# Softmax chain, layer-norm lead and 512-column weight splits in a two-layer decoder trunk

## The chip, the cores and the metric

The kernel runs on one core of one Trainium2 chip. The metric is the device time of one launch in microseconds (us), as the median of several runs. A profiled execution adds a trace; the numbers in the rows below come from that one execution.

## The reference

Two layers over one sequence of 512 tokens with 1024 features, all float32. Cut to what is computed:

```python
u = rmsnorm(x, g_pre)                                   # layer 0
z, xbc, dt_raw, q, k, v, f_raw = split(u @ e_w_in)      # 1024 x 7200
xbc = silu(causal_depthwise_conv(xbc, conv_w) + conv_b) # 4 taps -> xs, B, C
y = ssd_chunked(xs, dt, a, B, C) + xs * d_skip          # 4 groups, chunks of 128
y = group_rmsnorm(y * silu(z_ssd)) * ssd_norm
o = softmax(q k^T / 8 + c_t - c_s, causal) @ v          # 16 heads of 64
x = x + rmsnorm(concat(y, o * silu(z_fox)) @ e_w_out, g_post)

u = rmsnorm(x, g_pre)                                   # layer 1
val, gate, z = split(u @ o_w_in)                        # 1024 x 6144
h = causal_depthwise_conv(val * sigmoid(gate), w31) + b # 31 taps, 2048 channels
h = silu(layernorm(h, g, b)) * silu(z)
x = x + rmsnorm(h @ o_w_out, g_post)
```

## The kernel before

**Every product is made of three matmuls.** Each float32 operand is split in a rounded part (type fp32r, "hi") and the remainder ("lo"); `mm3` (L109) sums hi*hi, hi*lo and lo*hi. The rounding is a copy on ScalarE (ACT) and the remainder a subtract on VectorE (DVE) or GpSimd (POOL): `split` (L117) and `hilo` (L121).

**Weight jobs.** The two input projections and the two output projections are a list of jobs, each with 1024 columns' worth of weights in a 128x1024 tile. A job's weights go through three steps: `wload` (L159) loads a raw tile, of which there are two, with a DMA issued on SyncE's queue (SP); `cast` (L151) rounds it on ACT (L155 or L157 in the profile); a subtract on `j.eng` (L119 in the profile, tile name `w`) makes the lo part. `split_to` (L246) does this at priority offset 100 for the jobs up to two ahead of the running one, more where the dictionary `ahead` has an entry. A job's weights lie in a tile of pool `q` (7 buffers), or, where `j.small` is set, in four 128x512 tiles of pool `t` (56 buffers). By default jobs alternate between DVE and POOL; jobs 6 to 39 are all given to POOL (L1486), and jobs 0 to 3 are split before that. The 48 weight jobs of layer 1's input projection have their lo parts made long before, by `lo_ahead` (L190): load to `pre`, round on ACT to `prh` (L204), subtract on DVE (L205), store to DRAM. That filler is spread over layer 0 and its tiles are 128x1024.

**What sets the order.** TensorE (PE) runs its instructions in the order written. The queues of DVE, ACT and POOL are filled by the Tile framework's planner: it steps through a modelled time and takes, among the instructions that it holds ready on an engine, the one that is earliest in the program, with `tc.high_priority(offset=n)` counted as n places earlier. On the chip each queue then runs strictly in that order, so an instruction whose input is late holds back all that stand behind it. `HP` is 601 and is used before the change for the short convolution's taps, the SSD segments and some PSUM copies, not for attention.

**Layer 0.** Jobs 0 to 2 (B, C and x of group 0) run in two halves of 256 tokens as the tokens' norm comes in (L1094 to L1119). Then z and the other projections run; `Steps` (L270) puts SSD and attention steps between their matmuls when enough modelled PE time has passed since their inputs (DL, L1214, and the numbers in `attention`). In SSD, `bc_parts` (L1226) makes hi and lo of B and C, which `cbT` (L1267, PE tile `cb`) multiplies; later `states`, `state_parts` and `yoff` (PE tile `yo`) carry the state over chunks, and `gate_scale` (L1359, DVE L1362) feeds the transposes `yT`. In attention, for each of 16 heads and 4 query blocks, `sa` (L1421) writes logits to a PSUM bank `s`, then DVE takes the negated row maximum `nmx` (L1431), ACT the exponential with its row sum (tile `pr`, shown as L95), DVE the reciprocal `ri` (L1436), and POOL multiplies (L1437). `sb` (L1441) transposes that on PE (`pT`), and a split on ACT and DVE (`ph`, `pl`) feeds `sc`, the product with v. `sb` may follow `sa` after 8 us of modelled PE time. All eight PSUM banks come from one pool.

**Layer 1.** After the convolution 16 tiles of results lie in SBUF (`cvo`). The last three jobs of the input projection are z jobs of 24 matmuls each (tiles 13 to 15). `stats1` (L1032) stands before them: sums over channels on PE (`st`), mean and rstd on DVE and POOL, and diagonal tiles `dm` (L1049). `run(NZ[0])` runs some z jobs, `stats2` (L1051) broadcasts mean and rstd to two PSUM banks (`mu`, `rs`), `leads[1]()` runs the lead-in, and `run(NZ[1])` runs the z jobs left. NZ is [2, 1]. Then the output projection `out_proj` (L611) takes the 16 tiles in order (8 jobs for columns 0 to 511, of two tiles each, then 8 for the rest). Each tile goes through `lnorm` (DVE L1061 and L1062, then Silu on ACT), `lgate` (POOL L1067) and `hilo` (ACT, then DVE, tile `hll`). LA, LB and LC say how many tiles each of the three stages is ahead of PE; the lead-in fills them to that depth.

Of the kernel before, what the change touches and what calls it, by code (L numbers as in the profile page):

```python
# [36 lines left out]
def trunk(  # L37
# [21 lines left out]
    ctx.enter_context(tc.manual_schedule(engines={mybir.EngineType.PE}))  # L59

    HP = 601
    LA = 5
    LB = 4
    LC = 2
    NZ = [2, 1]
    GLO = [3, 11]
    uid = [0]

# [48 lines left out]
    def split(hi, lo, src, hi_eng, lo_eng):  # L117
        hi_eng(hi, src)
        lo_eng.tensor_tensor(lo, src, f32(hi), ALU.subtract)  # L119
# [57 lines left out]
    def wsplit(j):  # L177
        _, _, nk, _, n = j.spec
        hl = j.hl if j.lo is not None else wtiles(j.small)
        w = 1024 // len(hl[0])  # L180
        for i in range(len(hl[0])):
            src = j.raw[:, i * w : (i + 1) * w]
            if j.lo is not None:
                cast(hl[0][i], src)
            else:
                split(hl[0][i], hl[1][i], src, cast, j.eng)
        m = w // n
        return [lambda k, t=t: t[k // m][:, k % m * n : (k % m + 1) * n] for t in hl]

    def lo_ahead(js):  # L190


        def load(j):
            w, r0, nk, c0, n = j.spec
            t = ep.tile([P, 1024], F32, tag="e", name=nm("pre"))
            with tc.issue_after(last_load[0]):
                nc.sync.dma_start(t.rearrange("p (k f) -> p k f", k=nk),
                                  w[r0 : r0 + nk * P, c0 : c0 + n].rearrange("(k p) f -> p k f", p=P))
            return t

        def sub(t):
            h = eh.tile([P, 1024], F32R, tag="eh", name=nm("prh"))
            with tc.issue_after(last_cast[0]):
                A.copy(h, t)  # L204
            V.tensor_tensor(t.bitcast(F32R), t, f32(h), ALU.subtract)  # L205

        def store(j, t):
            j.lo = lop.tile([P, 1024], F32, tag="lo", name=nm("lo"))
            nc.sync.dma_start(j.lo, t)
        loaded = []  # L210
        for i in range(len(js) + 2):
            if i > 1:
                sub(loaded[i - 2])
            if i > 2:
                store(js[i - 3], loaded[i - 3])
            if i < len(js):
                loaded.append(load(js[i]))
            yield
        store(js[-1], loaded[-1])
# [869 lines left out]
        if b == 2:  # L1089
            load_to(2)  # L1090
    load_columns()
    jobs[0].eng, jobs[1].eng = V, G
    with tc.issue_after(mark["sq"]), tc.issue_after(mark["rstd"]), tc.issue_after(mark["scale"]):
        split_to(1)  # L1094
    to_uT(uh, ul, 0, us[0:2], c0)
# [129 lines left out]

    def bc_parts(g):  # L1226
        st = SG[g]
        st["B"] = hilo(st["Bf"], eng=G)
        st["C"] = hilo(st.pop("Cf"), eng=G)

    def x_tokens(g, i):

# [184 lines left out]
    def attention(steps):  # L1417
# [3 lines left out]
        def sa(h, i):  # L1421
# [5 lines left out]
            mm(ps[:, :L], QS[:, qs], KS[:, :L], True, False)  # L1427
            mm(ps[:, :L], QX[0:68, qs], KX[0:68, :L], False, False)
            mm(ps[:, L - P : L], identb, maskq, False, True)
            nmx = col("nmx")  # L1430
            V.tensor_reduce(nmx, ps[:, :L], AX.X, ALU.max, negate=True)  # L1431
            p = pr[h, i] = t2("pr")
            rs = col("rs")
            act(p[:, :L], ps[:, :L], AF.Exp, bias=nmx, accum_out=rs)
            ri = col("ri")
            V.reciprocal(ri, rs)  # L1436
            G.tensor_scalar(p[:, :L], p[:, :L], ri, 1.0, ALU.mult, ALU.mult)  # L1437
            if i == NB - 1:
                del qk["q", h], qk["k", h]

        def sb(h, i):  # L1441
# [4 lines left out]
            for kb in range(i + 1):  # L1446
                tr(pb[:, tok(kb)], p[:, tok(kb)], ident)
            src = pb.rearrange("p (k q) -> p k q", k=NB)[:, : i + 1, :]
            split(ph[h][:, : i + 1, tok(i)], pl[h][:, : i + 1, tok(i)], src, A.copy, V)

        def sc(h):
            po = bank("o")
# [51 lines left out]
        jobs[J1 + i].eng = V if i % 2 else G  # L1504
    for i in range(8):
        ahead[J1 - 8 + i] = max(2, min(NSMALL, 3 + 2 * (i - 2)) + 7 - i)
    run(J1 - state["run"])
    for _ in early:
        pass
# [59 lines left out]
```

## Time and profile before

| what | value |
|---|---|
| runs | 957.57, 959.45, 960.0 us; median 959.45 |
| the profiled execution | 954.4 us, its span 952.5 us, mean granted clock 0.989 |
| PE busy | 911.9 us (96%) |
| DVE busy | 736.3 us (77%) |
| ACT busy | 594.5 us (62%) |
| POOL busy | 503.3 us (53%) |
| HBM read, written | 129.45 MB, 29.36 MB |

The span runs from the first to the last instruction; the 1.9 us around it belong to the execution's own time. The profiled execution is 5.05 us shorter than the median of the runs. Matmuls are pipelined: a record of 0.39 us is the life of one matmul, and the pace is read from how many start in a stretch. [...]

### The profile page before, as it was taken

The page shows a single profiled execution, that of the slowest core. Times are in us where ns is not written, and L with a number is a line of the kernel's source. Part 1 is how long each engine was busy: PE and PEld are TensorE (multiplying, and loading weights), DVE is VectorE, ACT ScalarE, POOL GpSimd, SP SyncE. Part 2 cuts the span into 40 slices and gives each one's busy share as a digit, 9 for nine tenths or more (in the row PEclk, how much of TensorE's full clock was granted, in tenths as well). Part 3 has the DMA queues.
Part 4 walks back from the last instruction along what each step waited for, and adds up shares of the span by engine and source line. Part 5 has one row for each costly group of instructions (what it writes and reads, how often), then busy time and mean ns, then how long its engine had stood idle before and what let it go on. Part 6 is the DMA issues. An engine that isn't in the chain of part 4 may idle for free.

```text
span 952.5 us, 13693 instructions
## 1 busy us (share of the span) xinstructions
PE 911.9 (96%) x4691; PEld 757.7 (80%) x4691; DVE 736.3 (77%) x1220; ACT 594.5 (62%) x1073; POOL 503.3 (53%) x425
## 2 busy tenths in 40 slices
PE   5998999998999999989899999999999999998997
PEld 5976787886798888878678889888888887776885
DVE  5776967899887797968866257899999989769703
ACT  5547566575864766667585346788786778545500
POOL 2516443633632543434473202898999999458510
PEclk9999999999999999989999999999999999999999
DMA  6636522347774475664527793654664763513413
GB/s 186 193 106 198 169 75 67 89 133 243 222 241 135 134 245 187 190 200 138 173 90 243 243 367 152 189 165 146 221 208 136 231 188 124 170 72 133 147 52 110
DMA packets 180265, 159.83 MB, mean 168 GB/s; under 512 B 7708, under 2 KB 151716, under 8 KB 180196
## 3 DMA queue, kind: packets, MB, share of 16 engines
q1 hardware_dynamic: 180180, 158.96, 52.0%
q8 instruction: 37, 0.61, 0.2%
q14 instruction: 32, 0.26, 0.1%
q10 hardware_dynamic: 16, 0.00, 0.0%
HBM read 129.45 MB, written 29.36 MB: 167 GB/s over the span
## 4 chain that ended last, share of the span: by engine, by line
PE 69%; DVE 11%; issue 6%; ACT 5%; POOL 4%; DMA 3%; SPq 1%; DVEq 0%; POOLq 0%; ACTq 0%
PE m L102 39%; PE o L102 17%; PE tm L102 5%; POOL w L119 3%; DMA wr<-in_e_w_in_dram 2%; PE s L102 2%; DVE pre L205 2%; ACT w L157 2%; DVE hll L119 2%; PE pT L106 1%; PE yd L102 1%; PE acc L102 1%; DVE w L119 1%; DVE cvo L1062 1%; DVE cvo L1061 1%
## 5 line engine op out<-in xcount | busy, mean ns | idle before, releaser
L102 PE MATMUL m<-uh,w 128*128 128x512 f32 (+1 forms) x1392 | 452.7, 392 | 1.8 <-POOL w L119 1.8
L102 PEld LDWEIGHTS m<-uh,w 128*128 128x128 f32 x1392 | 260.8, 189 | 52.8 <-issue 3.1
L102 PE MATMUL m<-ul,w 128*128 128x512 f32 (+1 forms) x696 | 267.0, 384 | 0.0
L119 POOL TENSOR_TENSOR w<-wr,w 128x1024 fp32r<-128x1024 f32 x61 | 150.3, 2467 | 188.5 <-ACT w L157 151.0
L963 DVE SCALAR_TENSOR_TENSOR acc<-h,cw,acc 128x490 f32<-128x490 f32 (+14 forms) x272 | 177.6, 726 | 5.4 <-ACT acc L955 4.5
L102 PE MATMUL o<-w,hlh 128*128 128x512 f32 x512 | 160.9, 396 | 1.3 <-ACT pr L95 1.2
L870 POOL TENSOR_TENSOR acc<-acc,prod 128x505 f32<-128x505 f32 (+12 forms) x122 | 156.4, 1284 | 9.2 <-ACT prod L856 1.8
L102 PEld LDWEIGHTS m<-ul,w 128*128 128x128 f32 x696 | 132.0, 190 | 20.8 <-issue 0.5
L102 PEld LDWEIGHTS o<-w,hlh 128*128 128x128 f32 x512 | 94.5, 189 | 20.6 <-ACT pr L95 1.7
L102 PE MATMUL o<-w,hll 128*128 128x512 f32 x256 | 100.9, 394 | 4.9 <-DVE hll L119 4.9
L205 DVE TENSOR_TENSOR pre<-pre,prh 128x1024 fp32r<-128x1024 f32 x48 | 75.0, 1563 | 38.6 <-ACT prh L204 26.9
L157 ACT CAST w<-wr 128x1024 fp32r<-128x1024 f32 x72 | 75.1, 1048 | 46.3 <-DMA wr<-in_e_w_out_dram 18.8
L1437 POOL TENSOR_SCALAR pr<-pr,ri 128x128 f32<-128x128 f32 (+1 forms) x64 | 41.7, 653 | 104.4 <-DVE ri L1436 84.3
L102 PE MATMUL tm<-w,uh 128*128 128x256 f32 (+1 forms) x384 | 94.3, 337 | 1.7 <-ACT pr L95 1.7
L155 ACT CAST w<-wr 128x1024 fp32r<-128x1024 f32 x60 | 62.0, 1049 | 30.6 <-DMA wr<-in_o_w_out_dram 17.0
L856 ACT ACTIVATE prod<-h,cw 128x505 f32<-128x505 f32 (+12 forms) x122 | 77.7, 708 | 0.0
L102 PEld LDWEIGHTS tm<-w,uh 128*128 128x128 f32 x384 | 64.9, 196 | 7.6 <-ACT pr L95 1.9
L341 POOL TENSOR_TENSOR rstd<-var,mhalf 128x1 f32<-128x1 f32 (+1 forms) x20 | 12.8, 642 | 103.3 <-DVE var L339 103.1
L204 ACT CAST prh<-pre 128x1024 fp32r<-128x1024 f32 x48 | 50.4, 1050 | 21.5 <-DVE pre L205 19.6
L102 PE MATMUL tm<-w,ul 128*128 128x256 f32 (+1 forms) x192 | 62.5, 326 | 0.0
L102 PEld LDWEIGHTS o<-w,hll 128*128 128x128 f32 x256 | 48.4, 189 | 17.2 <-DVE hll L119 7.3
L95 ACT ACTIVATE pr<-s,nmx 128x128 f32<-128x128 f32 (+1 forms) x64 | 33.8, 529 | 36.3 <-DVE nmx L1431 22.9
(263 smaller groups left out, 1564.9 us busy)
## 6 DMA issues: line engine op xcount, KB each, us to landing
wr<-in_e_w_in_dram SPq DMA_DIRECT2D x56, 512.0 KB
pre<-in_o_w_in_dram SPq DMA_DIRECT2D x48, 512.0 KB
lo<-pre SPq DMA_DIRECT2D x48, 512.0 KB
wr<-in_o_w_in_dram SPq DMA_DIRECT2D x48, 512.0 KB
w<-lo SPq DMA_DIRECT2D x44, 512.0 KB
wr<-in_e_w_out_dram SPq DMA_DIRECT2D x16, 512.0 KB
wr<-in_o_w_out_dram SPq DMA_DIRECT2D x16, 512.0 KB
x<-in_x_dram SPq DMA_DIRECT2D x12, 256.0 KB
```

Source lines behind the costliest of these rows:

```text
L95: i = A.activation(*a, **kw)
L102: T.matmul(o, l, r, start=start, stop=stop, skip_group_check=True)
L119: lo_eng.tensor_tensor(lo, src, f32(hi), ALU.subtract)
L155: last_cast[0] = A.copy(hi, src).ins
L157: last_cast[0] = A.copy(hi, src).ins
L204: A.copy(h, t)
L205: V.tensor_tensor(t.bitcast(F32R), t, f32(h), ALU.subtract)
L341: mark["rstd"] = G.tensor_tensor(r, v, mhalf.to_broadcast([P, ss.shape[-1]]), ALU.pow).ins
L856: A.activation(prs[i][:, s:], hs[j][:, : S - s], AF.Copy, scale=w31(30 - s, j))
L870: G.tensor_tensor(a2[j][:, s:], a2[j][:, s:], prs.pop(i)[:, s:], ALU.add)
L963: V.scalar_tensor_tensor(a[:, s:], h[:, : S - s], w31(30 - s, j), a[:, s:], ALU.mult, ALU.add)
L1437: G.tensor_scalar(p[:, :L], p[:, :L], ri, 1.0, ALU.mult, ALU.mult)
```

## The change

```diff
-    LA = 5
-    LB = 4
-    LC = 2
-    NZ = [2, 1]
+    LA = 6
+    LB = 5
+    LC = 3
+    NZ = [1,2]
...
             else:
-                split(hl[0][i], hl[1][i], src, cast, j.eng)
+                cast(hl[0][i], src)
+                for c in range(0, w, S if j.eng is G else w):
+                    sl = slice(c, c + (S if j.eng is G else w))
+                    j.eng.tensor_tensor(hl[1][i][:, sl], src[:, sl], f32(hl[0][i])[:, sl], ALU.subtract)
...
         def sub(t):
             h = eh.tile([P, 1024], F32R, tag="eh", name=nm("prh"))
-            with tc.issue_after(last_cast[0]):
-                A.copy(h, t)
-            V.tensor_tensor(t.bitcast(F32R), t, f32(h), ALU.subtract)
+            for i in range(2):
+                sl = slice(i * S, i * S + S)
+                with tc.issue_after(last_cast[0]):
+                    A.copy(h[:, sl], t[:, sl])
+                V.tensor_tensor(t.bitcast(F32R)[:, sl], t[:, sl], f32(h)[:, sl], ALU.subtract)
...
-    jobs[0].eng, jobs[1].eng = V, G
+    jobs[0].eng, jobs[1].eng = V, V
...
     def bc_parts(g):
         st = SG[g]
-        st["B"] = hilo(st["Bf"], eng=G)
-        st["C"] = hilo(st.pop("Cf"), eng=G)
+        eng = G if g else V
+        st["B"] = hilo(st["Bf"], eng=eng)
+        st["C"] = hilo(st.pop("Cf"), eng=eng)
...
-            nmx = col("nmx")
-            V.tensor_reduce(nmx, ps[:, :L], AX.X, ALU.max, negate=True)
...
-            G.tensor_scalar(p[:, :L], p[:, :L], ri, 1.0, ALU.mult, ALU.mult)
+            with tc.high_priority(offset=HP):
+                nmx = col("nmx")
+                V.tensor_reduce(nmx, ps[:, :L], AX.X, ALU.max, negate=True)
+                p = pr[h, i] = t2("pr")
+                rs = col("rs")
+                act(p[:, :L], ps[:, :L], AF.Exp, bias=nmx, accum_out=rs)
+                ri = col("ri")
+                V.reciprocal(ri, rs)
+                G.tensor_scalar(p[:, :L], p[:, :L], ri, 1.0, ALU.mult, ALU.mult)
...
-            split(ph[h][:, : i + 1, tok(i)], pl[h][:, : i + 1, tok(i)], src, A.copy, V)
+            with tc.high_priority(offset=HP):
+                split(ph[h][:, : i + 1, tok(i)], pl[h][:, : i + 1, tok(i)], src, A.copy, V)
...
+    for i in range(4):
+        jobs[JO1 + i].small = True
+    for i in range(2, 8):
+        jobs[JO1 + i].eng = V
+    ahead[JO1 - 3], ahead[JO1 - 2], ahead[JO1 - 1], ahead[JO1] = 3, 4, 4, 4
     run(J1 - state["run"])
```

JO1 is the first job of layer 1's output projection. Its first eight jobs alternated between DVE and POOL before; now jobs JO1+2 to JO1+7 are all on DVE. The first four have their weights in 512-column tiles of pool `t`. The four entries of `ahead` let `split_to` reach one to two jobs further during the last three z jobs and the first output job. A subtract of 1024 weight columns on POOL becomes two of 512; on DVE it stays whole, except that a small job's tiles are 512 columns on either engine.

## Rows read from the trace of the kernel before

**Rows 1.** The page: span, and busy time and share of each engine.
```profile
span 952.5 us, 13693 instructions
PE 911.9 (96%) x4691; PEld 757.7 (80%) x4691; DVE 736.3 (77%) x1220; ACT 594.5 (62%) x1073; POOL 503.3 (53%) x425
```

**Rows 2.** PE's waits: waiter, what ended them, us in total, times, longest.
```profile
PE o L102 <- DVE hll L119: 4.9, 4, 2.1
PE yT L106 <- DVE y L1362: 3.5, 3, 2.0
PE cb L102 <- POOL hll L119: 3.5, 1, 3.5
...
PE yo L102 <- DVE hll L119: 2.3, 1, 2.3
PE m L102 <- POOL w L119: 1.8, 1, 1.8
PE tm L102 <- ACT pr L95: 1.7, 1, 1.7
...
PE pT L106 <- POOL pr L1437: 1.6, 2, 1.1
PE o L102 <- ACT pr L95: 1.2, 1, 1.2
PE s L102 <- DVE os L1463: 1.2, 1, 1.2
```

**Rows 3.** Windows at half clock: length, busy us (instructions) by engine, PEclk, DMA, GB/s.
```profile
88.69:92.10 3.41, 3.41 (x9) 1.94 (x8) 3.41 (x5) 1.19 (x3) 2.16 (x2) 0.50 0.87 251
232.05:235.46 3.41, 2.84 (x10) 2.27 (x10) 3.23 (x5) 1.18 (x2) 0.00 (x0) 0.50 0.93 262
409.54:416.37 6.83, 5.77 (x28) 5.19 (x27) 5.55 (x14) 3.47 (x9) 4.55 (x5) 0.50 0.91 285
467.57:470.98 3.41, 3.41 (x11) 2.25 (x11) 2.30 (x8) 1.91 (x7) 2.58 (x5) 0.50 0.08 22
```

**Rows 4.** Timeline of DVE and POOL, first group: start, us, instruction, idle before.
```profile
9.50 1.23 DVE L119 TENSOR_TENSOR w<-wr,w 128x1024 fp32r<-128x1024 f32 x1 [0.53 <-ACT w L157]
...
18.14 2.96 DVE L360 TENSOR_SCALAR x<-x,rstd 128x512 f32<-128x512 f32 x2 [0.73 <-POOL rstd L341]
...
18.07 2.34 POOL L119 TENSOR_TENSOR w<-wr,w 128x1024 fp32r<-128x1024 f32 x1
```

**Rows 5.** Timeline of DVE and POOL before the first `cb`.
```profile
82.36 3.44 DVE L205 TENSOR_TENSOR pre<-pre,prh 128x1024 fp32r<-128x1024 f32 x1 [1.12 <-ACT prh L204]
...
82.36 2.36 POOL L119 TENSOR_TENSOR w<-wr,w 128x1024 fp32r<-128x1024 f32 x1
84.68 2.25 POOL L119 TENSOR_TENSOR hll<-cv,hlh 128x512 fp32r<-128x512 f32 x1
```

**Rows 6.** Timeline of PE and DVE, one attention block's logits and their maximum.
```profile
399.30 0.28 PE L102 MATMUL s<-KS,QS 128*128 128x256 f32 x1
...
407.21 0.40 DVE L1431 TENSOR_REDUCE nmx<-s 128x1 f32<-128x256 f32 x1
```

**Rows 7.** Timeline of DVE, layer 1's statistics, lead-in and output projection.
```profile
835.26 0.88 DVE L1049 TENSOR_SCALAR dm<-ident,rstd 128x128 f32<-128x128 f32 x4 [0.36 <-POOL rstd L1045]
...
845.30 1.28 DVE L1061 TENSOR_TENSOR cvo<-cvo,mu 128x512 f32<-128x512 f32 x2 [3.49 <-PE mu L102]
...
864.96 2.85 DVE L119 TENSOR_TENSOR hll<-s,hlh 128x512 fp32r<-128x512 f32 x1
```

**Rows 8.** The chain that ended last: start, us, what; three z jobs.
```profile
815.30 16.34 PE m L102 x72
```

**Rows 9.** The page's groups: count, busy us, mean ns, idle before.
```profile
L119 POOL TENSOR_TENSOR w<-wr,w 128x1024 fp32r<-128x1024 f32 x61 | 150.3, 2467 | 188.5 <-ACT w L157 151.0
L205 DVE TENSOR_TENSOR pre<-pre,prh 128x1024 fp32r<-128x1024 f32 x48 | 75.0, 1563 | 38.6 <-ACT prh L204 26.9
```

**Rows 10.** Timeline of POOL: two subtracts of 512 columns.
```profile
459.02 2.71 POOL L119 TENSOR_TENSOR hll<-yT,hlh 128x512 fp32r<-128x512 f32 x2 [4.92 <-PE o L102]
```

More of the change, by code (lines that the diff above doesn't have):

```diff
@@ L1429, in sa @@
             mm(ps[:, L - P : L], identb, maskq, False, True)
-            nmx = col("nmx")
-            V.tensor_reduce(nmx, ps[:, :L], AX.X, ALU.max, negate=True)
[L1432 to L1436, printed above, removed]
-            G.tensor_scalar(p[:, :L], p[:, :L], ri, 1.0, ALU.mult, ALU.mult)
+            with tc.high_priority(offset=HP):
[7 more added lines that the diff above has]
+                G.tensor_scalar(p[:, :L], p[:, :L], ri, 1.0, ALU.mult, ALU.mult)
             if i == NB - 1:
```

## The prediction

> **What bounds the kernel now.** I read the page first: PE is busy 911.9 of 952.5 us, the others at most 77% [rows 1]. So there are two things to gain: the 40 us in which PE stands, and the time in which it runs slowly. PE's waits say what ended the standing, by name; five sorts touch this change: the output projection on the lo part (`o <- hll`, 4.9 us in four waits), `cb` on POOL's lo part (3.5), the first group on POOL's weights (1.8), and attention on its softmax chain (`tm`, `pT`, `o`, `s`: 1.7 + 1.6 + 1.2 + 1.2 = 5.7); `yT` (3.5) and `yo` (2.3) are neighbours [rows 2]. [...] In all the rest PE starts a 512-column matmul each 16.34/72 = 0.227 us and nothing in this change touches that pace [rows 8].
>
> **First group (job 1's subtract from POOL to DVE).** POOL takes 2.34 us from 18.07, behind a wait for the tokens' rstd that it also has to compute, and PE stands 1.8. Beside it DVE's two scales take 2.96 us [rows 2, 4]. On DVE the same subtract is 1.23 [rows 4]. It can run before 18.1, where DVE stood 0.73 us waiting, and then ends near 18.7 instead of 20.41; or behind the two scales, near 20.2. So 0.2 to 1.8; I take 1.4, since DVE is idle when the cast ends. What follows (x in two halves, z) depends on loads whose raw buffer is freed by this same subtract, so it moves with it.
>
> **bc_parts(0) on DVE.** `cb` waits for a lo part of 512 columns that POOL makes in 2.25 us (84.68 to 86.93) after a whole weight subtract of 2.36 that stood ahead of it [rows 5]. On DVE such a piece is 0.64 (1.28 for two) [rows 7]. DVE has the filler `pre` beside it, 3.44 us where its own mean is 1.56, because it overlaps POOL's 2.36: two-input work of the two engines ran one after the other here [rows 5, 9]. Before that filler the parts are there when PE comes, behind it some 2 us late. Gain 1.5 to 3.5 of wait, and with the full gain the half-clock stretch behind it, 1.7. Next late is `yo`, 30 us on, whose DVE chain doesn't start earlier by as much as PE: its 2.3 us can grow by what was won. Bounds 0 to 7.5 (3.5 + 1.7 + 2.3); I take 3.5, nearer the row of the wait itself.
>
> **512-column pieces.** POOL's 61 weight subtracts of 2.47 become pairs; the nearest row has two pieces at 2.71, so +0.24 each and at most 15 us of POOL in all [rows 9, 10]. POOL idled 188.5 us before just these instructions, so I count nothing. DVE's 48 fillers become pairs of 0.64, against 1.23 for one whole subtract without company: +0.05, 2.4 us in all [rows 4, 7, 9]; ACT's casts likewise. What hides it: the filler has no reader before layer 1, and DVE is idle 23% of the span. If that cover is missing in the DVE-heavy SSD stretch, it costs those 2.4 at most. The gain: whoever is locked out waits for a piece of about 1.3 instead of 2.4. The filler's mean excess, 1.56 - 1.23 = 0.33 on each of 48, shows how often this happens. It matters for PE where a chain is late: `yT` waits 3.5 us on DVE's scale and loses 1.4 to the clock. One lock-out halved is 1.2; bounds 0 to 4.9; I take 1.5.
>
> [...]
>
> **Softmax at priority 601.** A block's logits were written at 399.30 and their maximum taken at 407.21, 7.9 us later, on an engine that needs 0.40 us for it [rows 6]. In between DVE did evacuations, weight subtracts and fillers, any of which may now stand behind. The chain itself (maximum, exponential, reciprocal, product, some 2 us) fits in the 8 us that `sb` grants. Its price is the 5.7 us of waits and 2.9 + 1.7 of half clock behind them: 10.3 [rows 2, 3]. What is pushed back: `pre` (no reader), weight subtracts (two jobs ahead, 2 x 24 x 0.227 = 10.9 us of cover), evacuations of q and k (9 us of cover by `Steps`, but each holds a PSUM bank). I take 8 of 10.3, leaving one wait and no clock step; if the planner holds `pre` ready before the logits, and a load comes late on the chip, the queue is as before and the gain is 0.
>
> **Layer norm one z job sooner, leads one longer.** `dm` is complete at 836.14 and the broadcast on PE comes only after the second z job, so that DVE stands 3.49 us and starts at 845.30 [rows 7]. After one z job the broadcast comes 5.45 us sooner with all its inputs there. DVE then has two z jobs, 10.9 us, before the output projection begins: the longer lead-in needs 12 + 3 subtracts or products of 0.64, 9.6 us. From there DVE needs per output job 4 + 2 of them and one weight subtract of 1.23: 5.1 us against PE's 5.45. Before, POOL did half of the weight subtracts at 2.4 or more, and a lo part took 2.85 us beside one [rows 7]; now POOL keeps the gate alone. So the 4.9 us of waits go [rows 2]. Three more weight subtracts on DVE (3.7 us) are paid in the idle stretch before the lead-in, where `ahead` puts them. The 16 small tiles are the doubt: uh1, ul1 (16), cvo (16), sz (6), post gains (2) and three small jobs (12) hold 52 of 56 buffers at that time, and the lead-in's hi and lo want 6. It has to wait for the last z job, which frees two buffers per step. Bounds 0 to 4.9; I take 4.5.
>
> **Sum.** 1.4 + 3.5 + 1.5 + 8 + 4.5 = 18.9 us off the profiled execution's 954.4, so 935.5. That one stands 5.05 us under the median of the runs; I carry the difference over to it: 959.45 - 18.9 = 940.5.
>
> **Rivals.**
> (a) Half of it comes back. PE arrives earlier at chains that don't move as much (`yo`, `yT`, the transition to layer 1), or the planner's order lets the fillers stand where they stood. For: the waits have five different releasers on three engines, so each of them is nearly late. Against: the DVE idle time. Then first group 1, `cb` 1.5, attention 4, layer 1 3, sum 9.5: 950.
> (b) The edits change the order and no more: attention's waits shift to other blocks, small tiles starve the lead-in, and only the first group and part of `cb` remain, 1 to 3 us: 957.
> (c) Slower, by one mechanism: softmax in front holds up what frees PSUM. DVE runs strictly in order; a maximum queued before its logits are written keeps q and k evacuations behind it, PE finds no free bank or no weights, and the logits come later still. Its price by the nearest row is one wait of 1.2 us in each of 16 heads, 19 us, and two more clock steps of 1.7, while softmax's 8 us don't come: 959.45 - (18.9 - 8) + 22.6 = 971. With the clock steps it decides from 7 heads on: (10.9 - 3.4)/1.2 = 6.3. Against it: DVE's queue is late, not early, at the one block of rows 6.
>
> **How the numbers follow.** Forecast 0.58, with 932 to 947 as its own range; (a) 0.24; (b) 0.08; (c) 0.10. A difference under 0.3%, 2.9 us, is no change to this measurement: 956.6 to 962.3. Everything gained would be 1.8 + 7.5 + 4.9 + 10.3 + 4.9 = 29.4, so 930, and that is the low end; the high end is that of (a) with half of its gain lost again, 956, which leaves (b), (c) and little else out. Faster: 0.58 + 0.24 = 0.82; same: (b), 0.08; slower: (c), 0.10.
>
> **What would show it.** Right: no `m <- POOL w` and no `cb <- POOL hll` among PE's waits; the stretches at 0.50 near 90, 410 and 468 us gone; a maximum within 2 to 3 us of its logits; the mean of the filler's two halves together near 1.3; the broadcast after the first of three z jobs, and `o <- hll` under 1 us. Wrong: `yo` grown to 5 or more, new `m` waits on DVE's or ACT's weights or evacuations in attention (c), a lead-in that starts no sooner than the last z job, or POOL's pairs near 3 us.

## The result, and the profile after

The changed kernel takes 949.38 us (median of 18 runs, 947.6 to 953.18); 18 runs of the kernel before, among them, give 955.61 (950.38 to 962.18). The ratio is 0.9937, with a 95% interval of 0.9917 to 0.9957: 6.2 us or 0.6% less, where 18.9 were forecast. The forecast had counted from 959.45, the median of the first three runs of the kernel before; over 18 runs that median is 955.61.

Each run lists its span and mean granted clock. Span x (1 - clock) is what a kernel loses to the half clock, if PE is busy in it; span x clock is the rest, called the full-clock time below. Means over the runs:

| kernel | lost to the clock | full-clock time |
|---|---|---|
| before (23 runs of one series) | 16.1 | 939.2 |
| after (18 runs) | 10.6 | 937.4 |

The 23 runs are those beside e5_bc below. By these means most of the gain is clock, and only about 2 us are waits that went; in the other series below the kernel before loses 15.3 to 16.8 us and has 938.4 to 939.6 of full-clock time. First the page of the profile after: span, busy time by engine, and the two groups that answer to [rows 9].

```profile
span 949.2 us, 13869 instructions
...
PE 912.0 (96%) x4691; PEld 758.0 (80%) x4691; DVE 725.3 (76%) x1277; ACT 598.4 (63%) x1125; POOL 509.1 (54%) x476
...
L189 POOL TENSOR_TENSOR w<-wr,w 128x512 fp32r<-128x512 f32 x112 | 159.0, 1443 | 175.7 <-ACT w L157 122.7
...
L210 DVE TENSOR_TENSOR pre<-pre,prh 128x512 fp32r<-128x512 f32 x96 | 81.1, 863 | 43.8 <-ACT prh L209 43.7
```

PE is busy as long as before. PE's waits after (who waits, what ended it, us in total, times, longest), as [rows 2]:

```profile
PE uT L106 <- DVE x L365: 5.7, 2, 3.8
PE yT L106 <- DVE y L1368: 3.5, 5, 1.6
PE o L102 <- ACT hlh L118: 3.2, 1, 3.2
PE o L102 <- DVE hll L119: 2.9, 1, 2.9
...
PE m L102 <- DVE w L189: 2.2, 1, 2.2
...
PE o L102 <- ACT pr L95: 1.6, 2, 0.9
PE tm L102 <- ACT pr L95: 1.3, 1, 1.3
PE tm L102 <- DVE QS L589: 1.3, 1, 1.3
PE pT L106 <- POOL pr L1444: 0.7, 2, 0.5
```

`cb` and `yo` are gone. `m` waits for DVE instead of POOL, and longer. The two `o` rows of layer 1 are 6.1 us in two waits, where [rows 2] had 4.9 in four. Attention has 1.6 + 1.3 + 1.3 + 0.7 = 4.9 where 5.7 were counted. The windows at half clock, called clock steps below (length, then busy us and instructions of PE, PEld, DVE, ACT and POOL, PEclk, which is the granted share of TensorE's clock, DMA share, GB/s), as [rows 3]:

```profile
67.46:70.87 3.41, 3.41 (x9) 2.71 (x10) 0.68 (x1) 2.87 (x5) 0.00 (x0) 0.50 0.02 5
405.40:408.81 3.41, 3.09 (x13) 2.88 (x14) 3.20 (x8) 2.76 (x9) 1.07 (x2) 0.50 0.67 259
463.42:466.83 3.41, 3.41 (x11) 2.62 (x12) 2.37 (x6) 2.06 (x6) 1.35 (x3) 0.50 0.01 2
859.35:866.18 6.83, 5.02 (x12) 3.96 (x13) 6.83 (x9) 5.48 (x8) 3.87 (x3) 0.50 0.28 90
```

The stretch at 232 us is gone; the one at 89 is gone too, but one stands at 67, behind PE's wait of 2.2 us for `stk`. Both of attention are still there at the same blocks, one of them half as long, and a new one of 6.83 us stands in layer 1, behind the two `o` waits.

**Layer 1.** The lead-in starts where it was forecast: DVE's first subtract of `mu` is at 834.43 (845.30 in [rows 7]). What comes then is new. ACT, POOL and DVE after, timeline (start, us, instruction, idle before and what ended it):

```profile
827.67 1.14 ACT L155 CAST ws<-wr 128x512 fp32r<-128x512 f32 x2
...
843.58 2.18 ACT L155 CAST ws<-wr 128x512 fp32r<-128x512 f32 x4
...
853.71 1.14 ACT L155 CAST ws<-wr 128x512 fp32r<-128x512 f32 x2 [7.46 <-DMA wr<-in_o_w_out_dram]
...
857.40 0.82 ACT L95 ACTIVATE s<-cvo,c 128x512 f32<-128x512 f32 x1
```

```profile
837.30 9.15 POOL L1072 TENSOR_TENSOR s<-s,sz 128x512 f32<-128x512 f32 x6 [7.51 <-ACT s L95]
846.40 3.55 POOL L189 TENSOR_TENSOR ws<-wr,ws 128x512 fp32r<-128x512 f32 x2
```

```profile
849.91 0.68 DVE L1067 TENSOR_TENSOR cvo<-cvo,rs 128x512 f32<-128x512 f32 x1
854.36 0.69 DVE L189 TENSOR_TENSOR ws<-wr,ws 128x512 fp32r<-128x512 f32 x1 [3.78 <-ACT ws L155]
```

Read them as one chain. After the first small job's cast at 827.67 the next four small tiles are cast only at 843.58. POOL's subtract of them stands behind six gates of the lead-in (837.30 to 846.45) and ends at 849.95. Only that frees the raw tile for the next load, so the cast of the job after it reaches ACT's queue head before its data: ACT stands 7.46 us, and the Silu and `hlh` of tiles that PE needs stand behind that cast in the same queue, though nothing holds their own inputs. PE waits 3.2 and 2.9 us and then runs 6.83 us at half clock.

**Attention.** PE's and DVE's timeline after, the blocks ahead of the stretch at 405 us:

```profile
395.65 0.28 PE L102 MATMUL s<-KS,QS 128*128 128x256 f32 x1
```

```profile
400.36 0.69 DVE L589 SCALAR_TENSOR_TENSOR QS<-m,QS 64x512 fp32r<-64x512 f32 x1
401.08 0.42 DVE L590 CAST QX<-QS 64x512 fp32r<-64x512 f32 x1
401.42 0.68 DVE L210 TENSOR_TENSOR pre<-pre,prh 128x512 fp32r<-128x512 f32 x1
402.13 0.69 DVE L589 SCALAR_TENSOR_TENSOR QS<-m,QS 64x512 fp32r<-64x512 f32 x1
402.85 0.42 DVE L590 CAST QX<-QS 64x512 fp32r<-64x512 f32 x1
403.20 1.28 DVE L210 TENSOR_TENSOR pre<-pre,prh 128x512 fp32r<-128x512 f32 x2
404.40 0.15 DVE L1443 RECIPROCAL ri<-rs 128x1 f32<-128x1 f32 x1
404.58 0.42 DVE L1438 TENSOR_REDUCE nmx<-s 128x1 f32<-128x256 f32 x1
```

This block's logits begin at 395.65 and their maximum is taken at 404.58, 8.9 us later, with evacuations, that is copies of products out of PSUM and on (`QS`, `QX`), and fillers (`pre`) ahead of it in spite of a priority of 601 (7.9 us from the same start in [rows 6]). Over all 64 blocks the mean delay from the last matmul of the logits to their maximum is 2.78 us, 3.12 before.

### The profile page after: what moved, and what is told of

It reads as the page before. It is cut to its first block, busy times and chain, and to the rows that moved or that the text cites. A ratio compares the mean times of both kernels' runs of the same rounds, so it can differ in the third digit from the quotient of the medians.

```text
span 949.2 us, 13869 instructions
## 1 busy us (share of the span) xinstructions
PE 912.0 (96%) x4691; PEld 758.0 (80%) x4691; DVE 725.3 (76%) x1277; ACT 598.4 (63%) x1125; POOL 509.1 (54%) x476
## 4 chain that ended last, share of the span: by engine, by line
PE 69%; DVE 12%; DMA 6%; issue 5%; ACT 4%; POOL 3%; SPq 1%; DVEq 0%; POOLq 0%; ACTq 0%
PE m L102 40%; PE o L102 17%; PE tm L102 4%; DVE pre L210 2%; DMA wr<-in_e_w_in_dram 2%; POOL w L189 2%; PE yd L102 2%; PE s L102 1%; PE pT L106 1%; PE acc L102 1%; DMA lo<-pre 1%; DVE hll L119 1%; ACT w L157 1%; ACT pr L95 1%; DVE cv L512 1%
## 5 line engine op out<-in xcount | busy, mean ns | idle before, releaser
L189 POOL TENSOR_TENSOR w<-wr,w 128x512 fp32r<-128x512 f32 x112 | 159.0, 1443 | 175.7 <-ACT w L157 122.7
L102 PE MATMUL o<-w,hlh 128*128 128x512 f32 x448 | 141.1, 396 | 2.0 <-ACT pr L95 1.6
L210 DVE TENSOR_TENSOR pre<-pre,prh 128x512 fp32r<-128x512 f32 x96 | 81.1, 863 | 43.8 <-ACT prh L209 43.7
L157 ACT CAST w<-wr 128x1024 fp32r<-128x1024 f32 x72 | 75.1, 1049 | 47.1 <-DMA wr<-in_e_w_in_dram 20.8
L102 PEld LDWEIGHTS o<-w,hlh 128*128 128x128 f32 x448 | 82.7, 189 | 18.5 <-ACT pr L95 2.2
L102 PE MATMUL tm<-w,uh 128*128 128x256 f32 (+1 forms) x384 | 93.9, 336 | 2.6 <-ACT pr L95 1.3
L102 PE MATMUL o<-w,hll 128*128 128x512 f32 x224 | 87.8, 392 | 0.0
L1444 POOL TENSOR_SCALAR pr<-pr,ri 128x128 f32<-128x128 f32 (+1 forms) x64 | 39.6, 620 | 89.5 <-DVE ri L1443 73.2
L209 ACT CAST prh<-pre 128x512 fp32r<-128x512 f32 x96 | 56.6, 622 | 38.4 <-DVE pre L210 19.0
L155 ACT CAST w<-wr 128x1024 fp32r<-128x1024 f32 x56 | 57.8, 1048 | 26.8 <-PE o L102 9.8
L189 DVE TENSOR_TENSOR w<-wr,w 128x1024 fp32r<-128x1024 f32 x28 | 39.1, 1398 | 22.1 <-ACT w L157 19.4
```

The lines of the kernel that those rows point to most:

```text
L102: T.matmul(o, l, r, start=start, stop=stop, skip_group_check=True)
L155: last_cast[0] = A.copy(hi, src).ins
L157: last_cast[0] = A.copy(hi, src).ins
L189: j.eng.tensor_tensor(hl[1][i][:, sl], src[:, sl], f32(hl[0][i])[:, sl], ALU.subtract)
L209: A.copy(h[:, sl], t[:, sl])
L210: V.tensor_tensor(t.bitcast(F32R)[:, sl], t[:, sl], f32(h)[:, sl], ALU.subtract)
```

## Experiments

Ratios are to runs of the kernel before on the same chip in the same series (medians 954.1 to 958.0), with 95% intervals. Where two experiments come from different series, a difference of their medians and one of their ratios need not agree.

### Undoing one part at a time

**e1_nosoft**: after, without the priority around softmax and its split.

```diff
-            with tc.high_priority(offset=HP):
+            if True:
                 nmx = col("nmx")
...
-            with tc.high_priority(offset=HP):
+            if True:
                 split(ph[h]...
```

> The changed kernel with the softmax chain and the split of its transpose back at their old priority. Theory: the priority hardly moved the chain (mean delay from logits to maximum 3.12 us before, 2.78 after), because the planner's modelled time has the fillers ready before the logits; then this run is within 3 us of the changed kernel's 949.4, and the delay's mean stays between 2.5 and 3.3 us. Rival: the priority gave the 8 us of the prediction and another part lost them; then about 957, and the mean delay above 3.5.

Measured: 948.51 us, 0.9902 [0.9868, 0.9935]. Mean delay from logits to maximum 2.83 us against 2.78 with it. The priority did reorder (of the 348 instructions that DVE begins between 290 and 500 us at most 285 stand in the same sequence in both kernels), but brought nothing: without it the kernel is 0.9 us faster by the medians and 3.3 by the ratios, and the two intervals overlap. The priority has a price in the traces: the wait `tm <- DVE QS` of 1.3 us and the clock step at 405 are in those of after, e2_nosmall, e3_allV and e4_oldjobs, and in neither e1_nosoft nor e14_e4nosoft; in its place `o <- ACT pr` is longer there (3.0 and 2.5 us against 1.6).

**e2_nosmall, e3_allV, e4_oldjobs**: after without the small tiles; with all eight jobs on DVE; and with none of the three job edits.

```diff
-    for i in range(4):                # left out in e2, e4
-        jobs[JO1 + i].small = True
-    for i in range(2, 8):             # range(8) in e3, left out in e4
-        jobs[JO1 + i].eng = V
-    ahead[JO1 - 3], ... = 3, 4, 4, 4  # left out in e4
```

> The changed kernel with the first four output jobs of layer 1 in ordinary tiles of pool q instead of sixteen 512-column tiles of pool t. Theory: in the changed kernel the second and third job's casts stood until 843.6 us because pool t was full, so their raw tiles came free late (849.95), the next load landed at 853.7, and ACT's queue stood 7.5 us in front of that cast with the lead-in's Silu and casts behind it. Without small tiles the casts come before 840, the waits of 3.2 + 2.9 us and the half-clock stretch of 6.8 us go, and the time falls by 6 to 9, to 941 to 943. Rival: the late reload comes from POOL's subtract behind six gates; then the two waits stay and the time is within 2 us of 949.4.

> The changed kernel with all eight first output jobs of layer 1 subtracted on DVE, so that POOL has the gates alone. Theory (pool t full): casts still come at 843 or later, one raw tile is freed some 3 us sooner, the stall of 3.2 us shrinks but doesn't go: 1 to 3 us off 949.4. Rival (POOL's subtract behind the gates is the whole cause): the 7.5 us in which ACT stood go, 6 to 9 us off, 941 to 943.

> The changed kernel with the output jobs of layer 1 as before (alternating engines, tiles of pool q, two ahead), keeping the broadcast one z job sooner and the longer leads. If these two alone do what the prediction said, the 4.9 us of waits on the lo part fall under 1.5 and the time is 4 to 7 us under 949.4. If DVE or POOL run late without the moved subtracts, waits of 3 us or more on the lo part remain.

| kernel | median us | ratio | projection, first `o` to PE's end |
|---|---|---|---|
| after | 949.38 | 0.9937 [0.9917, 0.9957] | 96.2 |
| e3_allV | 947.24 | 0.9891 [0.9858, 0.9925] | 92.7 |
| e2_nosmall | 945.54 | 0.9873 [0.9839, 0.9906] | 90.7 |
| e4_oldjobs | 942.28 | 0.9842 [0.9804, 0.9879] | 87.2 |

The ideal is 384 matmuls at 0.227 us [rows 8], 87.2; before it was 93.9. So e4_oldjobs has no stall left there at all. Its ACT casts the job after the next with no wait, at the place where the changed kernel casts the small tiles 9 us later:

```profile
834.55 1.04 ACT L155 CAST w<-wr 128x1024 fp32r<-128x1024 f32 x1
```

Taking the small tiles away alone (e2) does the same to that cast (834.14) and removes the `hlh` wait and the clock step. The time falls by 3.8 us by the medians (6.1 by the ratios), not to 941 to 943: PE still waits 2.0 us for `hll`, in three waits, and the projection takes 90.7. Taking POOL's share away (e3) leaves the late cast where it was (843.47) and shortens ACT's stand to 5.58 us, as its theory said. The three job edits together cost 949.38 - 942.28 = 7 us (9 by the ratios), small tiles over half of it.

### One part alone

**e5_bc, e6_lead, e11_bclead**: the kernel before with `bc_parts(0)` on DVE; with the four constants LA, LB, LC and NZ; with both.

```diff
+        eng = G if g else V                       # e5, e11
-        st["B"] = hilo(st["Bf"], eng=G)
+        st["B"] = hilo(st["Bf"], eng=eng)
...
-    LA = 5 ... NZ = [2, 1]                        # e6, e11
+    LA = 6 ... NZ = [1,2]
```

> The kernel before with one edit: the lo parts of B and C of group 0 on DVE. Theory: this edit alone is the gain that the changed kernel shows between 85 and 150 us, the wait of cb (3.5) and that of yo (2.3) both gone: cb of group 1 near 145 us instead of 149.8, and 4 to 6 us less time. Rival 1 (the prediction's step): the yo wait takes back what cb wins, 3.5 or less. Rival 2: the gain is there at 150 us and lost again at the waits of yT near 230 and 285, time 1 to 2 us less.

> The kernel before with one edit: LA, LB, LC and NZ as in the change; layer 1's output jobs whole and alternating as before, no entries of ahead. Theory: the broadcast one z job sooner and the longer lead are all that layer 1 needed; no o <- hll and no o <- hlh among PE's waits, 87 to 88 us from the output projection's first matmul to PE's end (93.9 before), 5.5 to 7 us less time. Rival: the step needs the cheaper POOL pieces or the shorter layer 0 as well; 90 us or more for the projection and at most 4 us less time.

> The kernel before with two of the change's edits: bc_parts(0) on DVE, and LA, LB, LC and NZ. Theory: they add up, since one works at 85 to 115 us and the other after 830 us: full-clock time 5 to 6 us less and 5 us less lost to the clock, ratio 0.987 to 0.990, so better than the whole change (0.9937) with a fraction of it. Rival: the clock's part of bc_parts(0) was that kernel's chance; ratio 0.992 or more.

| kernel | median us | ratio | lost to the clock | full-clock time |
|---|---|---|---|---|
| before | 956.9 | | 16.1 | 939.2 |
| e5_bc | 950.28 | 0.9930 [0.9895, 0.9965] | 10.8 | 938.3 |
| e6_lead | 955.43 | 0.9972 [0.9939, 1.0005] | 17.7 | 934.6 |
| e11_bclead | 946.63 | 0.9894 [0.9851, 0.9936] | 10.2 | 934.5 |

The row of e11_bclead is of another series, whose kernel before has 956.89, 16.4 and 938.4.

e5_bc: in its trace `cb` of group 1 comes at 149.7 us, as before; rival 1 was right about the wait, which went from `cb` to `yo`:

```profile
PE yo L102 <- DVE hll L119: 2.6, 1, 2.6
```

Yet the time falls by 0.7%, and it falls in the clock: 5.3 of the 6.2 us. e6_lead shows how. Up to the third job from the end of layer 1's input projection its instructions on every engine and queue are those of the kernel before, in the same order, yet its profiled execution gets there 8.8 us later. Its windows at half clock:

```profile
87.20:107.68 20.48, 20.36 (x50) 13.88 (x51) 13.31 (x29) 8.06 (x13) 2.57 (x3) 0.50 0.51 171
124.74:128.15 3.41, 3.06 (x11) 2.87 (x12) 3.31 (x7) 0.47 (x1) 0.00 (x0) 0.50 0.95 279
```

The same wait ahead of `cb` (3.5 and 3.6 us) was followed by 3.41 us of half clock in one execution [rows 3] and by 20.48 in this one. The spread of the runs goes with that wait: with it, the kernel before spreads over 12.7 us in one series (clock 0.975 to 0.989) and e6_lead has 0.978 to 0.986; without it, the kernel after spreads over 5.6 (0.985 to 0.991), and e5_bc and e11_bclead have 0.985 to 0.991 and 0.987 to 0.991. Why the stretch is short in one execution and long in another stays open. The projection of e6_lead takes 87.7 us and its full-clock time is 4.6 less, nearly what was forecast, but by its time alone it can't be told from the kernel before. The sum e11_bclead adds up (0.9930 x 0.9972 = 0.9902): 946.63 with two edits, less than the whole change, though the intervals just meet. Its full-clock time is 4.0 under that of its own series, where 5 to 6 were expected.

**e7_whole**: e4_oldjobs with subtracts of 1024 columns, on POOL and in the filler.

```diff
-                for c in range(0, w, S if j.eng is G else w):
+                for c in range(0, w, w):
...
-            for i in range(2):
-                sl = slice(i * S, i * S + S)
+            for i in range(1):
+                sl = slice(0, 1024)
```

> The kernel without small tiles, V engines and ahead entries (e4_oldjobs), and with whole subtracts of 1024 columns on POOL and in the filler, as before the change. Theory: the pieces are worth little, 0 to 2 us; DVE's filler 48 instead of 96 instructions at about 1.56 us each, POOL's weights 61 at 2.47, ratio to the kernel before 0.984 to 0.987. Rival 1: pieces keep chains short, the stall and the half-clock step near 230 us come back, ratio 0.988 or more. Rival 2: pieces cost time at yT near 285 us (longer DVE queues), ratio 0.982 or less.

Measured: 947.16 us, 0.9892 [0.9841, 0.9944], against 0.9842 for e4_oldjobs: the pieces are worth about 5 us, though the two intervals overlap. Rival 1 was nearer. Its trace has the `yo` wait back and the stall at 230 us with its clock step:

```profile
PE yo L102 <- DVE hll L119: 2.3, 1, 2.3
```

```profile
230.10:236.93 6.83, 6.32 (x18) 4.87 (x19) 6.29 (x11) 4.10 (x6) 1.73 (x1) 0.50 0.74 230
```

DVE's own records show where the pieces help: its 1175 instructions beside the fillers are the same in both kernels and sum to 738.1 us in e7_whole and to 715.7 in e4_oldjobs. Rival 2 has a part in it too: e4_oldjobs has a clock step of 3.41 us at 285, behind waits of `yT`, and of the 8.5 us that it is ahead at the last `cb` 4.0 are left at the last `yT`. POOL's pieces and the filler's were not tried apart.

**e17_job1pool**: e14_e4nosoft (below) with job 1's subtract on POOL again.

```diff
-    jobs[0].eng, jobs[1].eng = V, V
+    jobs[0].eng, jobs[1].eng = V, G
```

> As e14_e4nosoft with job 1's subtract back on POOL, as before the change. Theory: on DVE that subtract stands behind the two scales (19.43 to 20.65 us in the changed kernel's trace), so the edit moved the wait from POOL to DVE and is worth 0: within 1.5 us of e14_e4nosoft, ratio 0.981 to 0.984. Rival (the prediction's step): 1.4 us or more slower, and the clock step near 67 us back near 88.

Measured: 940.11, 0.9836 [0.9795, 0.9878], against 939.90 (0.9824) with it on DVE: no difference that these runs can tell, though they could not tell 1.4 us either. The clock step stays near 67 (68.0). What decides is the trace of the kernel after; DVE's timeline:

```profile
18.63 0.88 DVE L365 TENSOR_SCALAR x<-x,rstd 128x512 f32<-128x512 f32 x2 [0.73 <-POOL rstd L346]
19.43 1.22 DVE L189 TENSOR_TENSOR w<-wr,w 128x1024 fp32r<-128x1024 f32 x1
```

The subtract ends at 20.65 behind the scales that the code makes it wait for; on POOL it ended at 20.41 [rows 4]. PE's wait for it is 2.2 us, 1.8 before.

### Why softmax in front brought nothing

**e8_nofill**: e4_oldjobs without the fillers' subtract on DVE; the raw weights are stored in place of their lo parts.

```diff
-                V.tensor_tensor(t.bitcast(F32R)[:, sl], t[:, sl], f32(h)[:, sl], ALU.subtract)
```

> As e4_oldjobs, but the filler's subtract on DVE is left out (the raw weights are stored in place of their lo parts; loads, casts on ACT and stores stay). Theory: fillers in front of the maxima are what priority 601 doesn't get past; without them attention's waits and its two half-clock stretches (405 and 463 us) go, the time from a block's logits to their maximum falls from 2.8 to under 1.5 us in the mean, and the time is 4 to 8 us under e4_oldjobs: ratio to the kernel before 0.976 to 0.980. Rival: evacuations of q, k and the pl parts hold up the maxima; the stretches at 405 and 463 stay and the ratio stays at 0.982 to 0.985.

Measured: 924.61 us, 0.9658 [0.9609, 0.9707]: 18 us less than e4_oldjobs, more than twice what the theory gave. Lost to the clock 2.6 (8.3 in e4_oldjobs), full-clock time 12 less. The mean delay from logits to maximum is 1.83 us, and the clock steps of attention are gone. All of PE's waits over half a us:

```profile
PE uT L106 <- DVE x L364: 6.7, 2, 4.9
PE pv L106 <- DMA v<-in_e_norm_pre_dram: 2.2, 1, 2.2
PE m L102 <- DVE w L189: 1.9, 1, 1.9
PE tk L106 <- DVE stk L1184: 1.4, 1, 1.4
PE o L102 <- ACT pr L95: 0.7, 1, 0.7
```

So the fillers do cause the stalls of SSD and attention. It is their own time in DVE's queue that does it: DVE's other 1175 instructions sum to 718.9 us here and to 715.7 in e4_oldjobs, so these got no shorter. The landmarks of PE say where: against e4_oldjobs 3 us are won by the last group's `yo` (265 us), 8 by the first `pT` (306), 18 by the last one (487). The next runs ask whether their order or their amount does it.

**e9_behind, e10_fillpool**: e4_oldjobs with each half of a filler's subtract forced behind the reciprocal of the last softmax block written before it; and with those subtracts on POOL.

```diff
-                V.tensor_tensor(t.bitcast(F32R)[:, sl], ...        # both
+                with tc.issue_after(last_ri[0] or last_cast[0]):   # e9
+                    V.tensor_tensor(t.bitcast(F32R)[:, sl], ...
+                G.tensor_tensor(t.bitcast(F32R)[:, sl], ...        # e10
```

> As e4_oldjobs, all of the computation in it, but each half of a filler's subtract has to stand behind the reciprocal of the last softmax block written before it in the program. Theory: what the change meant to do, done by an explicit order: fewer fillers in front of a maximum, delay from logits to maximum under 2.4 us in the mean (2.76 in e4_oldjobs), 2 to 6 us less time, ratio to the kernel before 0.978 to 0.982. Rival: DVE's total work in attention is what costs (26 of 30 us busy), and a filler put behind one block stands in front of the next; within 2 us of e4_oldjobs, ratio 0.982 to 0.986.

> As e4_oldjobs, all of the computation in it, but the filler's subtracts run on POOL (96 of 512 columns, about 1.44 us each, 138 us more for POOL, 81 us less for DVE). Theory: DVE's queue is what attention and yT wait for, so a good part of the 18 us that leaving the subtracts out was worth comes: 4 to 14 us under e4_oldjobs, ratio 0.970 to 0.980. Rival 1: POOL's product of softmax and its SSD parts now wait behind the fillers, and two-input work of POOL holds DVE up as in rows 5; within 3 us of e4_oldjobs or slower, pT <- POOL among PE's waits with over 3 us.

e9_behind: 945.58, 0.9887 [0.9838, 0.9935]; delay 2.97 us, not shorter. This order brought nothing either, as the rival said; it also put two fillers more into attention (23 instead of 21), so it is no test of order alone. e10_fillpool: 965.37, 1.0083 [1.0048, 1.0118], slower than the kernel before, though `pT <- POOL` is only 1.5 us. What got longer is on DVE; DVE's casts in attention, in e4_oldjobs and then in e10_fillpool (count, busy us, mean ns, idle before):

```profile
L590 DVE CAST QX<-QS 64x512 fp32r<-64x512 f32 x16 | 8.5, 530 | 0.5
L603 DVE CAST KS<-KS 64x512 fp32r<-64x512 f32 x16 | 8.1, 509 | 0.4
```

```profile
L590 DVE CAST QX<-QS 64x512 fp32r<-64x512 f32 x16 | 11.2, 700 | 0.4
L603 DVE CAST KS<-KS 64x512 fp32r<-64x512 f32 x16 | 10.6, 664 | 0.4
...
L210 POOL TENSOR_TENSOR pre<-pre,prh 128x512 fp32r<-128x512 f32 x96 | 132.9, 1398 | 37.6 <-ACT prh L209 36.2 <-DMA pre<-in_o_w_in_dram 0.5
```

The same casts take a third longer in the mean. The mean alone says little (642 and 777 ns in the kernel before); what it is made of says more. A cast with no POOL instruction beside it takes about 420 ns in both kernels; of the 16 `QX` casts 3 overlap one in e4_oldjobs (1012 ns in the mean) and 13 in e10_fillpool (765). In the traces of before and after together, 12 of these casts (`QX` and `KS`) begin inside a subtract on POOL; they take 910 to 2372 ns, and each ends 0.28 us after that subtract. One of them, DVE and POOL in the kernel before:

```profile
395.74 2.37 DVE L598 CAST KS<-KS 64x512 fp32r<-64x512 f32 x1
...
395.43 2.40 POOL L119 TENSOR_TENSOR w<-wr,w 128x1024 fp32r<-128x1024 f32 x1 [1.24 <-issue]
```

POOL is no free place for DVE's work: 83 us taken from DVE came back as 133 us on POOL, and DVE's other 1175 instructions sum to 745.6 us instead of 715.7.

**e12_thin, e13_thin2**: e4_oldjobs with fewer fillers per chunk of matmuls from job 26 on, and more in layer 0's output projection.

```diff
-                    if (8 * i + c) % (16 if i >= JO else 7 if i >= 26 else 8) == 0:
+                    if (8 * i + c) % (6 if i >= JO else 10 if i >= 26 else 8) == 0:   # 3 and 14 in e13
```

> As e4_oldjobs, all of the computation in it, but the filler is stepped every 10 instead of 7 chunks from job 26 on (second half of SSD, and attention) and every 6 instead of 16 in layer 0's output projection: about a third of the fillers move from 196-490 us to 490-565 us, where DVE is busy 24 of 60 us. Theory (the amount of DVE work in attention, not its order, sets the late maxima): 3 to 7 us less than e4_oldjobs, ratio to the kernel before 0.977 to 0.981, delay from logits to maximum 2.2 to 2.5 us. Rival 1: the order is what counts; nothing, 0.983 to 0.986. Rival 2: the moved loads and stores collide with the loads of layer 1's first weights near 560 us; PE waits for weights there and the time is 3 us or more above e4_oldjobs.

> As e12_thin with 14 and 3 in place of 10 and 6: half of the fillers moved. Theory: 6 to 10 us less than e4_oldjobs (half of the 18 that leaving all of the subtracts out was worth), ratio 0.974 to 0.978. Rivals as in e12_thin, rival 2 more likely here: waits for weights after 560 us.

e12_thin: 962.08, 1.0044 [1.0019, 1.0069]. e13_thin2: 969.58, 1.0124 [1.0092, 1.0156]. Both slower, and the traces show both halves of it. PE reaches the next-to-last group of `tm` at 395.1 and 393.5 us (402.8 in e4_oldjobs), with mean delays of 2.48 and 2.38. Of these 7.7 and 9.3 us, 5.9 and 7.1 are already there at attention's first `pT`, and 4.3 and 8.0 are left at the last block's `pT`: the delays shrink, the stage itself hardly does. Then all is lost, in e13_thin2 in part in layer 0's output projection (PE waits 10.6 us for weight casts), in e12_thin at the start of layer 1:

```profile
PE uT L106 <- DVE u L365: 22.0, 2, 11.2
```

```profile
564.30:588.19 23.89, 6.61 (x23) 5.74 (x24) 13.07 (x33) 9.53 (x24) 2.23 (x4) 0.50 0.97 335
```

The fillers left over run until 577 us, into a stretch with a DMA share of 0.97. It is not DVE's amount that costs here: DVE is busy 13.07 of 23.89 us. Its queue stands behind a filler, the filler behind its cast on ACT, and the cast behind a late load, with the norm of layer 1 behind them in both queues:

```profile
575.25 1.14 ACT L209 CAST prh<-pre 128x512 fp32r<-128x512 f32 x2 [5.53 <-DMA pre<-in_o_w_in_dram]
575.89 1.29 DVE L210 TENSOR_TENSOR pre<-pre,prh 128x512 fp32r<-128x512 f32 x2 [4.22 <-ACT prh L209]
```

That is the mechanism of layer 1's small tiles once more, and near to rival 2: late loads in a busy stretch, though what waited was the norm and not the weights.

**e14_e4nosoft, e15_mid16, e16_mid8**: e4_oldjobs without the priority; and that with some fillers moved into jobs 13 to 25 (110 to 196 us).

```diff
-            with tc.high_priority(offset=HP):         # all three, both places
+            if True:
...
-                if 5 <= i < 13 or 26 <= i:            # e15, e16
+                if 5 <= i:
-                    if (8 * i + c) % (16 if i >= JO else 7 if i >= 26 else 8) == 0:
+                    if (8 * i + c) % (16 if i >= JO else 8 if i >= 26 else 16 if i >= 13 else 8) == 0:   # e15; 10, 8, 8 in e16
```

> As e4_oldjobs without the priority around softmax. Theory: priority 601 changes the order and nothing else; within 2 us of e4_oldjobs, ratio 0.982 to 0.986, mean delay from logits to maximum within 0.3 us of 2.76. Rival: with layer 1's losses gone the priority is worth something; 3 us or more above e4_oldjobs.

> As e14_e4nosoft, all of the computation in it, but fillers are also stepped during jobs 13 to 25 (110 to 196 us, without any before), every 16 chunks, and every 8 instead of 7 chunks from job 26 on: some six of 48 fillers move from attention and SSD's second half to a stretch where DVE is busy 69 of 90 us and the DMA share is 0.2 to 0.44. Theory (amount per stage): what is won in attention isn't given back, because these loads and stores collide with nothing; 2 to 5 us under e14_e4nosoft, ratio to the kernel before 0.977 to 0.981. Rival: new waits of yT or yo on DVE between 120 and 200 us; within 1 us of e14_e4nosoft or above.

> As e15_mid16 with every 8 chunks for jobs 13 to 25 and every 10 from job 26 on: some 13 of 48 fillers moved. Theory: 4 to 8 us under e14_e4nosoft, ratio 0.974 to 0.978. Rival: DVE, at 24.5 of 30 us there already, gets 7.8 us more and becomes late between 150 and 196 us; waits of yT, yo or bc on DVE of 4 us or more, time above that of e15_mid16.

e14_e4nosoft: 939.90 (939.09 to 942.74), 0.9824 [0.9794, 0.9855], the lowest ratio of the kernels that leave nothing out: 1.8% under the kernel before. Its mean delay is 2.80 us. It can't be told apart from e4_oldjobs (0.9842), so no worth of the priority shows with layer 1 mended either. e15_mid16: 940.95, 0.9846 [0.9805, 0.9887], no gain: `yo` waits 2.1 us again and a clock step follows at 173 us. Two of the six fillers moved come out of attention, and its mean delay there is 3.20. e16_mid8: 946.74, 0.9910 [0.9876, 0.9943], worse, with 13.65 us of half clock from 171 us on and a wait of `yo` of 2.5 us at 225. Six fillers fewer in attention give a mean delay of 2.43 there, and more is lost before. The rivals held in the time, though no single wait of 4 us came. None of the places tried for this work was free.

## Why the prediction was wrong, step by step

| step | forecast us | measured us | from |
|---|---|---|---|
| job 1's subtract to DVE | 1.4 | 0 | its end in the traces; e17 against e14 can't tell |
| bc_parts(0) on DVE | 3.5 | 6 to 7, of which 5 clock | e5 against before |
| 512-column pieces | 1.5 | about 5 | e7 against e4 |
| softmax at priority 601 | 8 | 0, if not 1 to 3 lost | e1 against after, e14 against e4 |
| NZ and leads | 4.5 | 4.6 at full clock | e6 against before |
| small tiles, engines, `ahead` | 0 | 7 lost (9 by the ratios) | e4 against after |

The intervals above leave each of these uncertain by 3 to 5 us. Together they give some 8 us gained, against 6.2 measured. The 1.7, 1.4, 2.9 and 1.7 us that the forecast counts as lost to the clock are half of PE's busy time in the four windows at 0.50 of [rows 3], one execution; over 23 runs the kernel before lost 16.1 in the mean, and in e5_bc 5.3 of that went.

**Softmax at priority 601** is the step that failed. It took the 5.7 us of waits and the clock steps as the price of a wrong order, and one block's 7.9 us for the stage: over all 64 blocks the mean delay was 3.12 us, and 36 had their maximum within 2.5. In that stage DVE is busy 153 of 190 us in the kernel before, and what stands in front of a late maximum is mostly other work with a reader near: the 28 delays of over 2.5 us cover 73.7 us, of which DVE worked 68.1, and 16.0 of these on fillers. Four orders (before, after, e9_behind, e14_e4nosoft) gave mean delays of 2.8 to 3.1 us; less work gave 1.8 (e8_nofill) and 2.4 to 2.5 (e12_thin, e13_thin2, e16_mid8), though e15_mid16 with two fillers fewer has 3.20. And a shorter mean delay did not always shorten the stage: from the first to the last block's `pT` it is 181 us in e4_oldjobs, 171 in e8_nofill, 178 in e16_mid8, but 183 and 180 in e12_thin and e13_thin2. So the amount of work is the better account, and how much a fraction of it is worth stays open. Rival (a) named the outcome, "the planner's order lets the fillers stand where they stood", but not this reason for it: the order did change. That its 950 us lies within 1 us of the measured time is luck: its parts were 1, 1.5, 4 and 3, and it counted from 959.45. Of rival (c), evacuations held up by softmax, the traces show one wait, `tm <- DVE QS` of 1.3 us. That a filler has "no reader" made it look free. Leaving all of their subtracts out is worth 18 us, 10 of them in attention.

**Small tiles** are the other loss. The prediction counted 52 of 56 buffers of pool `t` taken, called this the doubt, and then priced it at nothing. The late casts of small tiles (843.58) against those of whole ones (834.14 in e2_nosmall) show the cost. That the full pool is what held them is what the count says; ACT did not stand just before 843.58, so the cast stood where the planner had put it, and no run here made the pool larger. The prediction also looked only for a late lead-in. The lead-in was early; late was the weight cast in front of it in ACT's queue, whose load waited for POOL, whose subtract waited behind the lead-in's own gates.

**bc_parts(0)**: the wait of `cb` moved to `yo` when done alone, as the prediction said that it might, and what was gained was the clock. It was priced at the 1.7 us of one profiled execution; the mean over runs is 5.

**Pieces** were worth more than one hold-up of DVE by POOL halved (the filler that took 3.44 us beside POOL's 2.36 [rows 5] is one): they also remove the `yo` wait and most of a stall at 230 us, and DVE's other instructions got 22 us shorter in all (e7_whole against e4_oldjobs). Their price was put too low, but it is hidden. The pairs on POOL take 2 x 1443 = 2886 ns against 2467 for a whole subtract [rows 9], 0.42 us dearer and not 0.24, and POOL still idles 175.7 us before them. The two halves of a filler take 2 x 863 ns against 1563 for a whole one, 163 dearer, where the prediction said 50; by busy time (81.1 against 75.0 us for 48) it is 127. The means hold times in which POOL worked beside them: without that a half takes 683 ns (54 of 96 after) and a whole 1218 (26 of 48 before), with it 1093 and 1972. Where two halves follow each other alone, they take 1.28 us (403.20 in the timeline above) against 1.23 for a whole [rows 4], as the prediction said.

**First group**: the bound of 0.2 was right, not the 1.4 taken: the subtract is held behind both scales, by an `issue_after` that the kernel had before, although DVE stood idle.

**NZ and leads** were right in size and mechanism: the broadcast comes 7.3 us after the statistics' first matmul instead of 12.7, and there is no `o <- hll` over 0.2 us in e6_lead.

The range itself has a slip: its high end of 956 was to be (a) with half of its 9.5 us lost again, which is 954.7.

## What to carry to other kernels

Before pricing a reorder, leave the suspected work out once and take the mean over all blocks, not one: here, with the engine busy four fifths of the stage, no order tried was worth anything and less work was. Count buffers before giving work smaller tiles in a pool that others hold, and follow the raw buffer round the ring (load, cast, subtract on another engine, next load), since one late member stopped a queue with ready work behind it here, 7.46 us in layer 1 and 5.53 in e12_thin. When the runs of a kernel spread, look at the granted clock of each run: an edit that removes one wait can be worth more in clock than in the wait (5.3 of 6.2 us in e5_bc).

## What was not expected of the hardware

- The same instructions after the same wait of 3.5 us were followed by 3.41 us of half clock in one execution and 20.48 in another, with PE busy 20.36 of them; over 23 runs the kernel before lost 16 us to the clock, and over 18 the changed one 10.6.
- DVE's `QX` casts of 64x512 took about 420 ns with no POOL instruction beside them, and 1012 (e4_oldjobs) and 765 ns (e10_fillpool) in the mean with one.
